# Five gate/up blocks of a hybrid decoder layer: shared products combined with one sum less, on a copied accumulator bank, and four summed pairs in each

## The chip, the cores and the metric

One core of one Trainium2 chip runs the whole layer as one program. The metric is the device time of one execution in microseconds (us); the kernel before took 1085.96 us, the median of three runs (1085.82 to 1085.98).

## What is computed

The reference is one decoder layer for 256 tokens of width 2048 in float32: a normalisation, one combined input projection, a gated linear recurrence beside eight retention heads, an output projection, and a SwiGLU feed-forward part of inner width 5632. The change lies in the feed-forward part:

```python
        h = h + jnp.einsum('bse,ed->bsd', y, w_out[l])
        u = rmsnorm(h, ln2_w[l])
        ff = jax.nn.silu(jnp.einsum('bsd,df->bsf', u, w_ffn_gate[l])) * jnp.einsum('bsd,df->bsf', u, w_ffn_up[l])
        h = h + jnp.einsum('bsf,fd->bsd', ff, w_ffn_down[l])
```

## The kernel before

Every weight is float32 and is split into a high and a low part that TensorE takes at its faster float32 rate (`split`, L110 to L113: ScalarE casts the high part at L112, VectorE subtracts it at L113 for the low part). A product of two split operands is three matmuls (`three`, L667 to L672). So TensorE multiplies three times for each product, and ScalarE and VectorE have to prepare two parts of every weight.

The output projection (blocks 0 and 1), the gate and up projections (blocks 2 to 12) and the down projection are cut into blocks. A gate/up block has two tiles of 128 tokens by two halves of 512 columns (512 gate columns and the matching 512 up columns), so four results, `c11`, `c12`, `c21`, `c22`, each a PSUM bank of 128x512. The depth of 2048 is cut into eight pairs of 128. For one pair the left side is a 2x2 of 128x128 pieces, `a11` to `a22`, and the weights are a 2x2 of 128x512 pieces, `b11` to `b22`.

A plain pair takes eight products (24 matmuls). A summed pair takes seven (21 matmuls), after Strassen and Winograd: VectorE makes four sums of the weight pieces (`Quad.add`, L644 to L648), and four of the seven products are added up over all summed pairs of the block before they are combined. These four are the shared products: `a11 b11`, `s1 t1`, `s3 t3` and `s2 t2`, in the banks `c11`, `c22`, `c21` and `c12` (`Block.share`, L771 to L787). After the last summed pair ScalarE copies the first out (L782), VectorE makes `p` and `q` (L783, L784), ScalarE writes `q` back to `c12` (L785), and VectorE rewrites `c22` and `c21` (L786, L787). Then the three direct products of each summed pair, whose weights are loaded a second time in half (`Direct`, L747), and the plain pairs accumulate onto the four banks.

Each block's work is a word of steps (`STEPS`, L36): `p` is a plain pair of the block itself, `d` the direct products of one of its own summed pairs, and `s` the shared products of one summed pair of the block that follows. So a block's four combined banks are ready before its own first step. `room` (L663) gives even and odd blocks four PSUM banks each in turn. After a block, two banks hold transposes of its result (`turn` in `ffn_post`, L828 to L835), which run during the next block's first step.

`SUMMED` (L32) names the summed pairs: block 3 has three, then 4, 3, 4, 3, 4, 3, 4 from block 4 to block 10, then three in blocks 11 and 12.

Loads go through SyncE's queue, 512 KB each, into six `raw` buffers; the split parts of plain and direct pairs, and of `t1`, `t3`, `b11`, `t2`, go to four pairs of buffers `wh`, `wl`. The program text is written in step order; a scheduler then puts each engine's instructions in an order of its own, and each engine runs its queue in that order. TensorE's rows therefore mix matmuls of two blocks.

Of the kernel before, what the change touches and what calls it, by code (L numbers as in the profile page):

```python
# [14 lines left out]
P = 128  # L15
D = 2048
S = 256
# [14 lines left out]
SUMMED = ((), (4, 5), (2, 3)) + ((1, 2, 3), (0, 1, 2, 3)) * 4 + ((1, 2, 3), (1, 2, 3))  # L32
# [3 lines left out]
STEPS = ("pppspppspp", "ppspdpsdpp", "pdpsdpspspp") + ("pspsdpsdpsdp", "psdpsdpsddp") * 4 + ("psdpsdpsdpp", "psdpsdpsdpp")  # L36


# [6 lines left out]
def tile_hymba_layer(ctx: ExitStack, tc: tile.TileContext, A: dict, out: bass.AP):  # L45
# [491 lines left out]
    class Left:  # L537
# [6 lines left out]
        def __init__(self, f, sums):  # L544
            self.h, self.l = [act_tile("ah", F32R)], [act_tile("al", F32R)]
            split(self.h[0], self.l[0], f)
            if sums:
# [4 lines left out]
                v.tensor_tensor(out=s2, in0=a11, in1=s1, op=ALU.add)  # L552
                v.tensor_tensor(out=s3, in0=a11, in1=a21, op=ALU.subtract)
                v.tensor_tensor(out=s4, in0=a12, in1=s2, op=ALU.subtract)
# [108 lines left out]
    def room(m):  # L663

        return (aux, bank)[m % 2]
# [56 lines left out]

    class Shared(Quad):


        hl = None, None

        def load(self, half):
# [4 lines left out]
            h, l = self.hl  # L733
            if half == 0:
                self.ra = r
                h, l = self.hl = [wpool.tile([P, 1024], F32R, tag=g, name=nm(g)) for g in ("wh", "wl")]
                self.parts["b11"] = h[:, :512], l[:, :512]
                split(*self.parts["b11"], r[:, :512])
                return
            self.add(r)  # L740
            self.parts["t2"] = h[:, 512:], l[:, 512:]
            split(*self.parts["t2"], r[:, :512])
            self.cut(("t1", "t3"), self.ra)
            self.parts["t4"] = act_tile("t4h", F32R), act_tile("t4l", F32R)
            split(*self.parts["t4"], r[:, 512:])
# [16 lines left out]
    class Block:  # L762


        def __init__(self, index, src, lefts, post, steps, summed, before=None):
            self.index, self.src, self.lefts, self.post, self.steps = index, src, lefts, post, steps
            self.summed = summed
            self.shared = [Shared(src(i), True, before and (lambda i=i: before(i))) for i in self.summed]
            self.ps = {}

        def share(self, m):  # L771
            left, right, last = self.lefts[self.summed[m]], self.shared[m].parts, m == len(self.summed) - 1
# [10 lines left out]
            v.tensor_tensor(out=p, in0=ps["c12"], in1=p1, op=ALU.subtract)  # L783
# [91 lines left out]
    def down_block(d, ahead):  # L875
# [15 lines left out]
        def post(c):  # L891
# [4 lines left out]
            elif c == "p7":  # L896
                n = act_tile("n")
                v.tensor_tensor(out=n, in0=ps["p6"], in1=ps["a1"], op=ALU.subtract)
# [303 lines left out]
```

## Time and profile before

| | |
|---|---|
| median of three runs | 1085.96 us |
| span of the profiled execution | 1084.4 us |
| TensorE busy | 1074.2 us (99%) |
| VectorE busy | 953.5 us (88%) |
| ScalarE busy | 660.9 us (61%) |
| first transposes of a block's result, from block 3 on | 437.6, 483.3, 521.7, 567.4, 605.7, 651.5, 689.8, 735.6 us |

The profiled execution's span, from its first to its last instruction, is 1.56 us under the median of the runs. PE is TensorE (PEld its weight loads), ACT ScalarE, DVE VectorE, SP SyncE. In a timeline the first column is the start in us from the span's start, the second the time in us until the end of the group, and the count of merged instructions stands at the end. A matmul's stated duration is from its start to its last result; the next one starts well before that. In the groups of instructions the columns behind the bar are busy time in us and the mean duration of one in ns.

### The profile page before, as it was taken

How to read it: one execution, taken by the hardware profiler on the slowest of the kernel's cores; microseconds unless marked ns; L12 is line 12 of the kernel's file. 1: busy time of each engine (PE TensorE's matmuls, PEld its weight loads, DVE VectorE, ACT ScalarE, POOL GpSimd, SP SyncE). 2: the span in 40 equal slices, each digit the busy share in tenths (PEclk: the TensorE clock that was granted, in tenths of full speed). 3: DMA queues.
4: the chain of work that ended last, by engine and by line, in shares of the span. 5: the costliest groups of instructions: out<-in, count | busy, mean ns of one | idle time of the engine just before them, and what ended most of it. 6: DMA issues, size and time to landing. Idle time of an engine off the chain costs nothing.

```text
span 1084.4 us, 14584 instructions
## 1 busy us (share of the span) xinstructions
PE 1074.2 (99%) x5101; PEld 899.5 (83%) x5101; DVE 953.5 (88%) x1371; ACT 660.9 (61%) x935; POOL 51.0 (5%) x61
## 2 busy tenths in 40 slices
PE   9999999999999999999999999999999999999997
PEld 7888888888888788888888888888888888888885
DVE  7789799988878889888998998999899899898986
ACT  7666644468746676565566566556556666655563
POOL 0612230000000000000000000000000000000001
PEclk9999999999999999999999999999999999999999
DMA  9964474444565567577677677686675756465652
GB/s 330 333 211 168 160 252 173 174 175 171 181 230 205 184 228 275 198 248 266 220 245 261 220 264 235 233 289 214 233 271 194 265 181 213 171 214 199 212 209 85
DMA packets 69274, 238.32 MB, mean 220 GB/s; under 512 B 7888, under 2 KB 8272, under 8 KB 69200
## 3 DMA queue, kind: packets, MB, share of 16 engines
q1 hardware_dynamic: 68400, 235.29, 62.7%
q0 software_dynamic: 512, 1.57, 0.4%
q8 instruction: 40, 0.66, 0.2%
q10 hardware_dynamic: 288, 0.52, 0.1%
q14 instruction: 34, 0.28, 0.1%
HBM read 235.26 MB, written 2.10 MB: 219 GB/s over the span
## 4 chain that ended last, share of the span: by engine, by line
PE 97%; DVE 1%; issue 1%; DMA 0%; ACT 0%; POOL 0%; SPq 0%; POOLq 0%; ACTq 0%
PE c L670 22%; PE c L672 22%; PE c L671 22%; PE fm L184 11%; PE fm L186 5%; PE tm L164 3%; PE tm L165 3%; PE tm L166 3%; PE p L672 1%; PE p L671 1%; PE p L670 1%; PE ft L833 1%; DMA raw<-in_w_v 0%; PE ht L576 0%; PE sc L482 0%
## 5 line engine op out<-in xcount | busy, mean ns | idle before, releaser
L112 ACT CAST wh<-raw 128x1024 fp32r<-128x1024 f32 (+1 forms) x490 | 460.9, 965 | 362.6 <-PE c L672 132.5
L113 DVE TENSOR_TENSOR wl<-raw,wh 128x1024 fp32r<-128x1024 f32 (+1 forms) x490 | 538.2, 1122 | 91.2 <-ACT wh L112 88.4
L671 PE MATMUL c<-wl,ah 128*128 128x512 f32 x850 | 331.0, 390 | 0.0
L672 PE MATMUL c<-wh,al 128*128 128x512 f32 x850 | 330.4, 389 | 0.0
L670 PE MATMUL c<-wh,ah 128*128 128x512 f32 x850 | 275.0, 391 | 0.2 <-ACT wh L112 0.2
L670 PEld LDWEIGHTS c<-wh,ah 128*128 128x128 f32 x850 | 159.4, 188 | 33.4 <-ACT wh L112 1.1
L672 PEld LDWEIGHTS c<-wh,al 128*128 128x128 f32 x850 | 159.6, 188 | 33.0
L671 PEld LDWEIGHTS c<-wl,ah 128*128 128x128 f32 x850 | 159.6, 188 | 32.7
L184 PE MATMUL fm<-u,wh 128*128 128x512 f32 x512 | 161.3, 396 | 0.0
L186 PEld LDWEIGHTS fm<-u,wl 128*128 128x128 f32 x512 | 96.0, 188 | 22.5
L186 PE MATMUL fm<-u,wl 128*128 128x256 f32 x512 | 101.1, 278 | 0.0
L184 PEld LDWEIGHTS fm<-u,wh 128*128 128x128 f32 x512 | 78.4, 189 | 0.3
L648 DVE TENSOR_TENSOR raw<-raw,raw 128x512 f32<-128x512 f32 x106 | 73.1, 690 | 2.8
L648 DVE TENSOR_TENSOR raw<-raw 128x512 f32<-128x512 f32 x106 | 72.7, 689 | 2.4
L671 PE MATMUL c<-wl,sh 128*128 128x512 f32 x176 | 68.5, 389 | 0.0
L672 PE MATMUL c<-wh,sl 128*128 128x512 f32 x176 | 68.0, 389 | 0.0
L670 PE MATMUL c<-wh,sh 128*128 128x512 f32 x176 | 60.4, 394 | 0.3 <-ACT sh L112 0.3
L165 PE MATMUL tm<-wl,u 128*128 128x512 f32 x128 | 48.8, 394 | 0.0
L166 PE MATMUL tm<-wh,u 128*128 128x512 f32 x128 | 48.7, 390 | 0.0
L164 PE MATMUL tm<-wh,u 128*128 128x512 f32 x128 | 47.3, 398 | 0.8 <-ACT u L288 0.8
L954 POOL TENSOR_TENSOR htok<-htok,fw 128x512 f32<-128x512 f32 x2 | 2.5, 1273 | 895.9 <-ACT junk L947 895.9
L670 PEld LDWEIGHTS c<-wh,sh 128*128 128x128 f32 x176 | 33.1, 188 | 7.3 <-ACT sh L112 0.7
(245 smaller groups left out, 1034.9 us busy)
## 6 DMA issues: line engine op xcount, KB each, us to landing
raw<-in_w_gu SPq DMA_DIRECT2D x212, 512.0 KB, 5.5
raw<-in_w_down SPq DMA_DIRECT2D x91, 512.0 KB, 4.3
raw<-in_w_out SPq DMA_DIRECT2D x34, 512.0 KB, 3.7
raw<-in_w_lx SPq DMA_DIRECT2D x16, 512.0 KB, 6.3
raw<-in_w_k SPq DMA_DIRECT2D x16, 512.0 KB, 3.5
raw<-in_w_q SPq DMA_DIRECT2D x16, 512.0 KB, 4.0
raw<-in_w_rg SPq DMA_DIRECT2D x16, 512.0 KB, 3.4
raw<-in_w_lg SPq DMA_DIRECT2D x16, 512.0 KB, 3.4
```

Of the source, the lines that this page charges most:

```text
L112: act.copy(out=dst_h, in_=src)
L113: v.tensor_tensor(out=dst_l, in0=src, in1=dst_h.bitcast(F32), op=ALU.subtract)
L164: pe.matmul(ps, ah, wh, start=first, stop=False)
L165: pe.matmul(ps, ah, wl, start=False, stop=False)
L166: pe.matmul(ps, al, wh, start=False, stop=last)
L184: pe.matmul(ps, wh, hl, start=n + i == 0, stop=False)
L186: pe.matmul(ps[:, :S], wl, hl[:, :S], start=False, stop=n + i == len(order) - 1)
L648: v.tensor_tensor(out=dst, in0=a, in1=b, op=ALU.add)
L670: pe.matmul(p, ah, bh, start=first, stop=False, skip_group_check=onto)
L671: pe.matmul(p, ah, bl, start=False, stop=False, skip_group_check=onto)
L672: pe.matmul(p, al, bh, start=False, stop=last, skip_group_check=onto)
L833: pe.transpose(pt[:, o : o + P], g[:, (2 * b + c) * P : (2 * b + c) * P + P], ident)
```

## The change

It sets four summed pairs in each of blocks 4 to 8 (blocks 5 and 7 had three), and forms the shared products of these five blocks in another way.

In these blocks (`KEEP`) the bank `c22` first takes `a11 b11` of the four summed pairs. After the last of these, ScalarE copies `c22` into a fourth bank, which becomes `c11`; that bank is the one that held the second of the transposes of two blocks earlier (`spare`). Then the four `s2 t2` products are added onto `c22` itself, all at the end, so the split `t2` of each pair is kept in two tiles until then. `s2` has its sign turned, so that `c22` holds the sum that VectorE made before at L783, with the other sign, and ScalarE reads it out as `p` with a scale of -1. The rest, `q` and the three rewrites, is as before. The order of VectorE's sums changes in all shared pairs: `t1`, `t3` are made and split first, then `t2`, then `t4`. In blocks outside `KEEP` the combining is as before, with a sign turned in one instruction (`share_apart`).

```diff
-SUMMED = ((), (4, 5), (2, 3)) + ((1, 2, 3), (0, 1, 2, 3)) * 4 + ((1, 2, 3), (1, 2, 3))
+SUMMED = ((), (4, 5), (2, 3)) + ((1, 2, 3),) + ((0, 1, 2, 3),) * 5 + ((1, 2, 3), (0, 1, 2, 3), (1, 2, 3), (1, 2, 3))
...
+KEEP = tuple(range(4, 9))
...
     class Shared(Quad):
...
+            if self.keep:
+                self.parts["t2"] = act_tile("t2h", F32R), act_tile("t2l", F32R)
             self.parts["t4"] = act_tile("t4h", F32R), act_tile("t4l", F32R)
-            split(*self.parts["t4"], r[:, 512:])
+            b11, b12, b22, b21 = self.ra[:, :512], self.ra[:, 512:], r[:, :512], r[:, 512:]
...
+            def second():
+                add(b12, b12, b22)
+                self.cut(("t1", "t3"), self.ra)
+
+            def third():
+                add(b22, b11, b22)
+                split(*self.parts["t2"], b22)
...
         def share(self, m):
...
+            for c, a, b in (("c22", "a11", "b11"), ("c12", "s1", "t1"), ("c21", "s3", "t3")):
+                if m == 0:
+                    ps[c] = room(self.index)(c)
+                three(ps[c], left[a], right[b], m == 0, last)
+                if last and c == "c22":
+                    ps["c11"], spare[self.index % 2] = seed, None
+                    act.copy(out=seed, in_=ps["c22"])
+            if not last:
+                return
+            for k, i in enumerate(self.summed):
+                three(ps["c22"], self.lefts[i]["s2"], self.shared[k].parts["t2"], False, i == self.summed[-1], True)
+
+            p, q = act_tile("p"), act_tile("q")
+            act.activation(out=p, in_=ps["c22"], func=AF.Copy, scale=-1.0)
+            v.tensor_tensor(out=q, in0=p, in1=ps["c12"], op=ALU.subtract)
+            act.copy(out=ps["c12"], in_=q)
+            v.tensor_tensor(out=ps["c22"], in0=q, in1=ps["c21"], op=ALU.subtract)
+            v.tensor_tensor(out=ps["c21"], in0=ps["c21"], in1=p, op=ALU.subtract)
...
         def turn(b):
             pt = room(j)("ft")
-            for c in range(2):
-                for t, g in enumerate(gated):
-                    o = c * S + t * P
-                    pe.transpose(pt[:, o : o + P], g[:, (2 * b + c) * P : (2 * b + c) * P + P], ident)
+            transposes(pt, [g[:, (2 * b + c) * P : (2 * b + c) * P + P] for c in range(2) for g in gated])
+            if b and j + 4 in KEEP:
+                spare[j % 2] = pt
```

The order of the instructions moves as follows. The places shown belong to block 6, which has four summed pairs before and after; its shared products run during block 5's steps. Numbers in the names are the scheduler's; in the kernel before block 6's banks are `c11_1091`, `c22_1092`, `c21_1093`, `c12_1094`, in the changed one `ft_1105` (the copied bank), `c22_1113`, `c12_1114`, `c21_1115`.

TensorE in the kernel before, around the last of block 6's shared products (the second row is the last `a11 b11`, the fourth the last `s2 t2`, the last but one the first later use of the bank that held `a11 b11`, the last row the first later use of `c22`):

```order
L671 MATMUL c11_1091_5278<-wl_1128_5452,ah_755_3715 128x512 [waits DVE_49]
L672 MATMUL c11_1091_5278<-wh_1127_5451,al_756_3716 128x512
...
L671 MATMUL c12_1094_5290<-wl_1128_5452,sh_758_3724 128x512 [waits DVE_49]
L672 MATMUL c12_1094_5290<-wh_1127_5451,sl_759_3725 128x512
L671 MATMUL c11_1018_4939<-wl_1139_5513,ah_845_4126 128x512 [waits DVE_49]
...
L670 MATMUL c11_1091_5278<-wh_1147_5545,ah_833_4090 128x512 [waits Activation_49]
...
L670 MATMUL c22_1092_5282<-wh_1147_5545,ah_833_4090 128x512 [waits DVE_49]
```

Between the second row and the last but one stand 31 matmuls, and between the fourth and the last row 26.

TensorE in the changed kernel, where block 6's last `a11 b11` (first three rows) meets its first `s2 t2` (fourth row):

```order
L672 MATMUL c22_1113_5326<-b11h_1149_5487,ah_755_3715 128x512 [waits Activation_49]
L673 MATMUL c22_1113_5326<-b11l_1150_5488,ah_755_3715 128x512 [waits DVE_49]
L674 MATMUL c22_1113_5326<-b11h_1149_5487,al_756_3716 128x512
L672 MATMUL c22_1113_5326<-t2h_1094_5254,sh_737_3661 128x512 [waits Activation_49]
L673 MATMUL c22_1113_5326<-t2l_1095_5255,sh_737_3661 128x512
```

No matmul stands between the third row and the fourth, which waits for ScalarE's copy of that bank. Blocks 7 and 8 have the same, with no matmul between; in block 4 it is 19, in block 5 it is 17.

ScalarE in the changed kernel at the same place; the second row is the copy, L825 is `p`:

```order
L114 CAST b11h_1149_5487<-raw_1148_5485 128x512 [waits DMAHW6_49]
L818 COPY ft_1105_5295<-c22_1113_5326 128x512 [waits PE_49]
L114 CAST wh_1156_5499<-raw_1148_5485 128x1024 [waits DVE_49,Activation_49]
L114 CAST wh_1159_5520<-raw_1158_5518 128x1024 [waits DMAHW0_49,Activation_49]
L114 CAST wh_1162_5535<-raw_1161_5533 128x1024 [waits DMAHW1_49,Activation_49]
L114 CAST wh_1165_5541<-raw_1164_5539 128x1024 [waits DMAHW2_49,Activation_49]
```

The casts of the last summed pair's `t1`, `t3` and of the next three loads stand behind the copy.

TensorE in the changed kernel at the end of the shared products (the second row is the last `s2 t2`) up to the first use of the rewritten `c22` (last row):

```order
L673 MATMUL c22_1113_5326<-t2l_1153_5494,sh_758_3724 128x512 [waits DVE_49]
L674 MATMUL c22_1113_5326<-t2h_1152_5493,sl_759_3725 128x512
L673 MATMUL ft_1105_5295<-wl_1171_5577,ah_833_4090 128x512 [waits DVE_49]
L674 MATMUL ft_1105_5295<-wh_1170_5576,al_834_4091 128x512
L672 MATMUL ft_1105_5295<-wh_1173_5591,ah_833_4090 128x512 [waits Activation_49]
L673 MATMUL ft_1105_5295<-wl_1174_5592,ah_833_4090 128x512 [waits DVE_49]
L674 MATMUL ft_1105_5295<-wh_1173_5591,al_834_4091 128x512
L672 MATMUL c22_1113_5326<-wh_1170_5576,ah_833_4090 128x512 [waits DVE_49]
```

Five matmuls stand between, where 26 stood. Block 7 has the same five; block 4 has 30, block 5 has 11, and in block 8 five matmuls are followed by a transpose that waits for VectorE.

VectorE in the kernel before, from the low parts of the last pair's `t1`, `t3` (first row) to the rewrite of `c22` (last row); the third row is the low part of `t2`:

```order
L113 TENSOR_TENSOR wl_1131_5473<-raw_1126_5449,wh_1130_5472 128x1024 [waits Activation_49]
L113 TENSOR_TENSOR wl_1136_5483<-raw_1134_5480,wh_1135_5482 128x1024 [waits DMAHW7_49,Activation_49]
L113 TENSOR_TENSOR wl_1128_5452<-raw_1129_5464,wh_1127_5451 128x512 [waits Activation_49]
L113 TENSOR_TENSOR t4l_1133_5477<-raw_1129_5464,t4h_1132_5476 128x512 [waits Activation_49]
L113 TENSOR_TENSOR wl_1139_5513<-raw_1137_5510,wh_1138_5512 128x1024 [waits DMAHW0_49,Activation_49]
L113 TENSOR_TENSOR wl_1142_5519<-raw_1140_5516,wh_1141_5518 128x1024 [waits DMAHW1_49,Activation_49]
L113 TENSOR_TENSOR wl_1148_5546<-raw_1146_5543,wh_1147_5545 128x1024 [waits DMAHW2_49,Activation_49]
L783 TENSOR_TENSOR p_1144_5535<-c12_1094_5290,p1_1143_5534 128x512 [waits PE_49]
L113 TENSOR_TENSOR wl_1151_5561<-raw_1149_5558,wh_1150_5560 128x1024 [waits DMAHW3_49,Activation_49]
L784 TENSOR_TENSOR q_1145_5536<-p_1144_5535,c22_1092_5282 128x512 [waits DVE_49]
L113 TENSOR_TENSOR wl_1154_5567<-raw_1152_5564,wh_1153_5566 128x512 [waits DMAHW4_49,Activation_49]
L786 TENSOR_TENSOR c22_1092_5282<-q_1145_5536,c21_1093_5286 128x512 [waits DVE_49]
```

VectorE in the changed kernel over the same stretch; the fifth row is the low part of the last `t2`:

```order
L115 TENSOR_TENSOR wl_1157_5500<-raw_1148_5485,wh_1156_5499 128x1024 [waits PE_49,Activation_49]
L115 TENSOR_TENSOR wl_1160_5521<-raw_1158_5518,wh_1159_5520 128x1024 [waits DMAHW0_49,PE_49,Activation_49]
L115 TENSOR_TENSOR wl_1163_5536<-raw_1161_5533,wh_1162_5535 128x1024 [waits DMAHW1_49,PE_49,Activation_49]
L115 TENSOR_TENSOR wl_1166_5542<-raw_1164_5539,wh_1165_5541 128x1024 [waits DMAHW2_49,PE_49,Activation_49]
L115 TENSOR_TENSOR t2l_1153_5494<-raw_1151_5491,t2h_1152_5493 128x512 [waits Activation_49]
L115 TENSOR_TENSOR wl_1171_5577<-raw_1169_5574,wh_1170_5576 128x1024 [waits DMAHW3_49,Activation_49]
L115 TENSOR_TENSOR t4l_1155_5496<-raw_1151_5491,t4h_1154_5495 128x512 [waits Activation_49]
L115 TENSOR_TENSOR wl_1174_5592<-raw_1172_5589,wh_1173_5591 128x1024 [waits DMAHW4_49,Activation_49]
L826 TENSOR_TENSOR q_1168_5568<-p_1167_5567,c12_1114_5330 128x512 [waits Activation_49]
L115 TENSOR_TENSOR b11l_1177_5598<-raw_1175_5595,b11h_1176_5597 128x512 [waits DMAHW5_49,Activation_49]
L828 TENSOR_TENSOR c22_1113_5326<-q_1168_5568,c21_1115_5334 128x512 [waits DVE_49]
```

The last `t2` has moved from behind two low parts of 128x1024 to behind four, and `q` stands at the end with one other instruction between it and the rewrite of `c22`.

In all, TensorE has six matmuls of 128x512 fewer. VectorE has eight sums and six subtractions of 128x512 more and five combining sums fewer. ScalarE has six casts of 128x512 and five copies more, and SyncE two loads more. Over its last 1762 rows TensorE's order is the same as before in everything but the numbers of the names, and over its first 2159 as well.

More of the change, by code (lines that the diff above doesn't have):

```diff
@@ L721, in block, with transposes @@
         program.append((quads[n:], end))
+    spare = [None, None]
+    def transposes(pt, parts):
+        for n, x in enumerate(parts):
+            pe.matmul(
+                pt[:, n * P : n * P + P], x, ident, start=n == 0, stop=True, is_transpose=True, skip_group_check=n > 0
+            )
     class Shared(Quad):
-        hl = None, None
+        keep = False
         def load(self, half):
```

42 lines of the change are left out of this document (30 added, 12 removed).

## Prediction

> **What bounds the kernel now.** I began with the page: its busy times and the chain of work that ended last.
>
> ```profile
> span 1084.4 us, 14584 instructions
> PE 1074.2 (99%) x5101; PEld 899.5 (83%) x5101; DVE 953.5 (88%) x1371; ACT 660.9 (61%) x935; POOL 51.0 (5%) x61
> ...
> PE 97%; DVE 1%; issue 1%; DMA 0%; ACT 0%; POOL 0%; SPq 0%; POOLq 0%; ACTq 0%
> ```
>
> The chain is TensorE's almost alone. A busy TensorE may still be a slow one, so I looked next at its waits and at the pace of its matmuls. First the waits of TensorE in the whole program (us in total, times, longest), then a piece of its timeline in block 4:
>
> ```profile
> PE warm L105 <- DVE eps_t L98: 1.1, 1, 1.1
> PE tm L164 <- ACT u L288: 0.8, 2, 0.5
> PE c L670 <- ACT sh L112: 0.3, 1, 0.3
> PE c L670 <- ACT wh L112: 0.2, 1, 0.2
> ```
> ```profile
> 519.15 0.39 PE L671 MATMUL c<-wl,ah 128*128 128x512 f32 x1
> 519.38 0.39 PE L672 MATMUL c<-wh,al 128*128 128x512 f32 x1
> 519.61 0.39 PE L670 MATMUL c<-wh,ah 128*128 128x512 f32 x1
> 519.83 0.39 PE L671 MATMUL c<-wl,ah 128*128 128x512 f32 x1
> ```
>
> TensorE waits 2.4 us in all, and nowhere in the blocks that change. Its matmuls start (519.83 - 519.15) / 3 = 0.227 us apart and each ends 0.39 us after its start. So a matmul less is worth 0.227 us, and a wait that TensorE does not have today is added to the time in full. Next the four stretches from block to block that hold the steps of blocks 4 to 7 (length, then busy us of PE, PEld, DVE, ACT), and the waits in the part of the program that the change reorders:
>
> ```profile
> 483.30:521.70 38.40, 38.40 (x175) 31.80 (x174) 34.23 (x42) 22.85 (x31) 0.00 (x0) 1.00 0.73 247
> 521.70:567.40 45.70, 45.70 (x207) 37.90 (x206) 41.86 (x52) 27.02 (x36) 0.00 (x0) 1.00 0.71 242
> 567.40:605.70 38.30, 38.30 (x174) 31.75 (x173) 34.14 (x42) 22.77 (x31) 0.00 (x0) 1.00 0.74 247
> 605.70:651.50 45.80, 45.80 (x207) 37.95 (x206) 41.96 (x53) 27.12 (x36) 0.00 (x0) 1.00 0.70 241
> sum 168.20, PE 168.20 PEld 139.41 DVE 152.20 ACT 99.76 POOL 0.00; mean PE 42.05 PEld 34.85 DVE 38.05 ACT 24.94 POOL 0.00
> ```
> ```profile
> ACT wh L112 <- DVE raw L648: 59.4, 22, 3.0
> ACT wh L112 <- PE c L672: 47.8, 42, 2.2
> DVE wl L113 <- ACT wh L112: 21.4, 18, 1.8
> ```
>
> TensorE is busy for the whole 168.20 us; VectorE, at 152.20 us (90%), is the next. ScalarE waits for TensorE 42 times: the two preparing engines run ahead and are held back by full buffers. They bound nothing now, but VectorE has only 16 us to spare here.
>
> **What the change takes away.** Blocks 5 and 7 have one plain pair less and one summed pair more: 24 matmuls become 21, twice. The sum is 6 x 0.227 = 1.4 us less, on the path.
>
> **What it adds beside other work.** The durations:
>
> ```profile
> L113 DVE TENSOR_TENSOR wl<-raw,wh 128x1024 fp32r<-128x1024 f32 x392 | 477.7, 1231 | 78.4 <-ACT wh L112 75.8
> L112 ACT CAST wh<-raw 128x1024 fp32r<-128x1024 f32 x392 | 406.5, 1052 | 324.8 <-DVE raw L648 113.2 <-PE c L672 100.3 <-PE fm L184 47.0
> L648 DVE TENSOR_TENSOR raw<-raw,raw 128x512 f32<-128x512 f32 x106 | 73.1, 690 | 2.8
> L113 DVE TENSOR_TENSOR wl<-raw,wh 128x512 fp32r<-128x512 f32 x98 | 66.9, 683 | 12.7 <-ACT wh L112 12.5
> L112 ACT CAST wh<-raw 128x512 fp32r<-128x512 f32 x98 | 60.4, 617 | 37.7 <-PE c L672 32.2 <-DMA raw<-in_w_v 3.6 <-issue 1.4
> L842 ACT ACTIVATE gated<-c,r_tok 128x512 f32<-128x512 f32 x22 | 13.9, 683 | 1.1 <-PE c L672 1.1
> L844 DVE SCALAR_TENSOR_TENSOR gated<-c,r_tok,gated 128x512 f32<-128x512 f32 x22 | 15.8, 741 | 0.6 <-ACT gated L842 0.6
> L786 DVE TENSOR_TENSOR c<-q,c 128x512 f32<-128x512 f32 x13 | 8.9, 686 | 0.0
> L785 ACT COPY c<-q 128x512 f32<-128x512 f32 x13 | 7.7, 589 | 1.6 <-DVE q L784 1.6
> L782 ACT COPY p<-c 128x512 f32<-128x512 f32 x13 | 7.5, 574 | 0.0
> ```
>
> VectorE gets 8 sums (0.69) and 6 subtractions (0.68) and loses 5 combining sums (0.69): 5.5 + 4.1 - 3.5 = 6.1 us more, against a TensorE that needs 1.4 us less. Put wholly into the four stretches this is 158.3 of 166.8 us, 95%: covered, with half the room left. ScalarE's six casts (0.62) and five copies (0.57 to 0.68) come to some 7 us on 100 of 168: covered. Two more loads of 512 KB ride on DMA engines that are busy 0.70 to 0.74 there: covered. The sign turned at L843 outside the five blocks costs VectorE at most 0.741 - 0.684 us in each of eight places: covered.
>
> **What it adds on the path.** TensorE runs its queue in order, so what counts is how many of its matmuls stand between a result and the first that needs it back through another engine. The steps of such a round trip, from two pieces of timeline (a cast that waited for TensorE and a subtraction that waited for the cast; a matmul that waited for a cast) and VectorE's own pace:
>
> ```profile
> 610.50 0.39 PE L672 MATMUL c<-wh,al 128*128 128x512 f32 x1
> ...
> 610.92 0.62 ACT L112 CAST wh<-raw 128x512 fp32r<-128x512 f32 x1 [2.13 <-PE c L672]
> ...
> 611.58 0.69 DVE L113 TENSOR_TENSOR wl<-raw,wh 128x512 fp32r<-128x512 f32 x1 [1.83 <-ACT wh L112]
> ```
> ```profile
> 370.78 0.61 ACT L112 CAST sh<-s 128x512 fp32r<-128x512 f32 x1
> ...
> 371.44 0.50 PE L670 MATMUL c<-wh,sh 128*128 128x512 f32 x1 [0.30 <-ACT sh L112]
> ...
> 371.78 0.39 PE L671 MATMUL c<-wl,sh 128*128 128x512 f32 x1
> ```
> ```profile
> 515.07 0.69 DVE L786 TENSOR_TENSOR c<-q,c 128x512 f32<-128x512 f32 x1
> 515.67 0.69 DVE L787 TENSOR_TENSOR c<-c,p 128x512 f32<-128x512 f32 x1
> 516.27 0.68 DVE L113 TENSOR_TENSOR wl<-raw,wh 128x512 fp32r<-128x512 f32 x1
> ```
>
> From TensorE's end to ScalarE 0.03, ScalarE to VectorE 0.04, ScalarE to TensorE 0.05; I take 0.05 for VectorE to TensorE too. VectorE starts instructions of this size 0.60 apart. After a wait the next two matmuls start 0.34 apart and not 0.227, so a wait costs 0.11 beside its length.
>
> *The copied bank.* The copy cannot start before the last `a11 b11` has ended, and the first `s2 t2` not before the copy has. From the start of the last matmul: 0.39 + 0.03 + the copy + 0.05. A copy from one PSUM bank to another is not in the trace; the nearest are into PSUM 0.589 and out of it 0.574, and I take 0.58. That makes 1.05, and TensorE would have gone on after 0.227: with the slower start 0.93 us lost. In blocks 4 and 5 the 19 and 17 matmuls between (over 4 us) cover it. In blocks 6, 7 and 8 none stands between: 3 x 0.93 = 2.8 us. What is queued behind the copy on ScalarE are four casts of 128x1024; the first `s2 t2` products are nine matmuls (2.0 us), the first cast is ready 1.05 us after the copy and its low part 1.23 later (2.3), needed at 2.9; the following casts come at 2.1 and 3.2 for needs at 2.5 and 3.9. So I count nothing more there.
>
> *The end of the shared products.* The last `t2`'s low part stands on VectorE behind four low parts of 128x1024, so the last `s2 t2` comes late in TensorE's order, after most other matmuls of that step. Then the chain runs: matmul's end 0.39, 0.03, `p`, 0.04, `q`, the low part of the next `b11`, the rewrite of `c22`, 0.05. `p` is a new form; its bounds are the copy, 0.574, and the ACTIVATE with a vector as scale, 0.683, and I take the copy's, since it has a constant scale. (The Trainium skill, "ScalarE: Activation LUTs", section "What ACT_TABLE_LOAD costs", gives an ACTIVATE with constant scale 186 ns and 0.833 ns an element, and 93 ns more for a vector operand. The rows agree in the difference, 0.683 against 0.589. By the rule `p` is an estimated 0.61, and the four chains that hang on it come to some 0.15 us more in all.) `q` starts at 1.03, the rewrite two starts of 0.60 later, and ends 0.69 after that: 2.92, and TensorE has it at 2.97. With n matmuls between, TensorE gets there at (n + 1) x 0.227. Block 4, n = 30: covered. Block 5, n = 11: 2.72, so 0.25 + 0.11 = 0.36. Blocks 6 and 7, n = 5: 1.36, so 1.61 + 0.11 = 1.72 each. Block 8: after five matmuls a transpose waits for the gating at L844, which is queued behind `q` and one sum: 1.03 + 0.60 + 0.7 + 0.74 + 0.05 = 3.12, so 1.87. Together 0.36 + 3.44 + 1.87 = 5.7 us. In the kernel before, the same chain had 26 matmuls over it.
>
> **The sum.** -1.4 + 2.8 + 5.7 = +7.1 us: the profiled span goes from 1084.4 to 1091.5, and the median, 1.56 above the span, from 1085.96 to 1093.1 us. The bounds: if the slower start after a wait falls away (seven times 0.11) and the VectorE instructions between cost nothing (four times 0.60), 3.2 us less, 1089.9.
>
> **The rivals.** *The waits are over when TensorE gets there* (not slower). The combination occurs 13 times in the kernel before, and TensorE never waited for it; if the engines' lead covered the round trips here as well, only the six matmuls would count: 1085.96 - 1.4 = 1084.6 us. It decides at the point where the rows between take longer than the trip, 1.05 us for the copy and 2.97 for the end. Against it: a lead helps with operands that can be made early, and these come out of TensorE's own last matmul; the rows between are 0 and 5. The Trainium skill, "TensorE: Matmul & The Clock Gate", Part 2, "Step-by-step: what each phase is for", says that TensorE's queue may pull weight loads ahead while the matmuls stay in program order. By that rule no later matmul fills the gap; the matmul that waited at 371.44 above, with nothing run in its place, agrees. Chance 7%.
>
> *VectorE becomes late as well* (slower still). At each copy ScalarE is held until TensorE is done, the lead of both preparing engines is used up, and at 95% VectorE does not win it back, so that TensorE also waits for low parts. If after each of the three uncovered copies one low part of 128x1024 comes a whole subtraction late, that is 3 x 1.23 = 3.7 us more: 1096.8 us. For it: the 16 us to spare halve. Against it: TensorE's own waits give VectorE 7 us back. Chance 15%.
>
> **How the numbers follow.** The forecast, waits of 5 to 9 us against 1.4 us, has 78%; its time is 1093.1. The range reaches from its lower bound, rounded down, to the second rival: 1089.5 to 1097.0. A difference under 0.2%, 2.2 us, cannot be told from none here. The first rival is 0.13% faster and counts mostly as the same: faster 3%, same 6%, slower 91%.
>
> **What would show it.** Right: TensorE's waits in the profile after have new rows, a wait of the first `s2 t2` for ScalarE's copy, three times, some 0.8 us each, and waits for VectorE's rewrite of `c22` in blocks 5, 6 and 7 and its gating in block 8; TensorE has 5095 matmul records or close to it; the stretches of blocks 4 to 8 hold the whole difference and the end of the program is as long as before. Wrong: TensorE without waits there (the first rival), or waits for low parts, `wl` at L115, that exceed those for the copy and the combination (the second).

## The result and the profile after

The changed kernel takes 1093.88 us (median of 4 runs, 1092.71 to 1096.22) beside 1085.97 us before (4 runs, 1085.82 to 1087.17): ratio 1.0075, 95% interval 1.0061 to 1.0089. A second set of five runs, with the experiments below, gave 1093.62 us and 1.0070 (1.0057 to 1.0082). It is slower by 8 us, and the forecast was 1093.1. The profiled run took 1092.71 us.

The page after, with the chain's shares by engine, and then TensorE's waits (us in total, times, longest):

```profile
span 1090.9 us, 14574 instructions
PE 1074.7 (99%) x5095; PEld 897.4 (82%) x5095; DVE 958.5 (88%) x1380; ACT 664.3 (61%) x946; POOL 50.9 (5%) x61
...
PE 96%; issue 1%; DVE 1%; ACT 1%; DMA 0%; POOL 0%; SPq 0%; POOLq 0%; ACTq 0%
```
```profile
PE c L672 <- DVE c L828: 3.0, 2, 1.5
PE c L672 <- ACT ft L818: 2.0, 3, 0.7
PE ft L730 <- DVE gated L903: 1.5, 1, 1.5
```

Six matmuls are gone, and three kinds of wait are new: for the rewrite of `c22` (L828), for the copy into the seed bank (L818), and for block 8's gating (L903). No wait for a low part (L115) has come. The rewrite shows twice here and not three times, since block 5's wait (0.13 us) is too short to be listed. The shares of the page hardly show them: TensorE stands at 99% in both kernels, 1074.7 of 1090.9 us and 1074.2 of 1084.4.

Where the time went is read from the stretches of the blocks that change. The first fence has three of the seven stretches between the first transposes of successive blocks, and the sum, in the changed kernel; the second has the sum of the same seven in the kernel before:

```profile
436.60:481.50 44.90, 44.90 (x204) 37.24 (x203) 40.92 (x51) 27.04 (x37) 0.00 (x0) 1.00 0.72 246
...
524.80:569.30 44.50, 42.36 (x190) 34.40 (x189) 39.59 (x50) 25.62 (x36) 0.00 (x0) 1.00 0.70 237
569.30:613.80 44.50, 42.36 (x189) 34.40 (x188) 39.56 (x50) 25.64 (x36) 0.00 (x0) 1.00 0.71 236
...
sum 305.80, PE 299.19 PEld 245.67 DVE 274.91 ACT 179.24 POOL 0.00; mean PE 42.74 PEld 35.10 DVE 39.27 ACT 25.61 POOL 0.00
```
```profile
sum 298.00, PE 298.00 PEld 247.04 DVE 269.67 ACT 176.21 POOL 0.00; mean PE 42.57 PEld 35.29 DVE 38.52 ACT 25.17 POOL 0.00
```

These stretches are 7.8 us longer: 8.4 us of waits, added up below, less five matmuls (1338 against 1343 records between the first transposes, 1.1 us); the 0.5 us that is left was not placed. What lies ahead of them was 1.0 us shorter (436.6 against 437.6). One matmul of that has moved across the boundary (0.2), and the rest belongs to this run: TensorE did not wait for `u`, as it had for 0.8 us in the trace before. The end is 0.3 us shorter (348.5 against 348.8): 6.5 us of span in all. The two stretches of 44.50 us hold the two full pairs of waits. Here is the copy's wait in block 6 (start, duration, engine, line, operation):

```profile
549.27 0.39 PE L674 MATMUL c<-b11h,al 128*128 128x512 f32 x1
549.70 0.57 ACT L818 COPY ft<-c 128x512 f32<-128x512 f32 x1 [4.61 <-PE c L674]
550.18 2.00 ACT L114 CAST wh<-raw 128x1024 fp32r<-128x1024 f32 x2
550.32 0.50 PE L672 MATMUL c<-t2h,sh 128*128 128x512 f32 x1 [0.66 <-ACT ft L818]
550.65 0.39 PE L673 MATMUL c<-t2l,sh 128*128 128x512 f32 x1
```

The last `a11 b11` starts at 549.27, the first `s2 t2` at 550.32 and not at 549.50: 0.82 late, and the next 0.11 later still. (The 0.66 in brackets counts from the end of the matmul before, 0.39 after its start, where the next would have started 0.227 after it. So a wait costs its bracket, 0.16, and the slower start of 0.11.) And the end of block 6's shared products:

```profile
561.34 0.39 PE L674 MATMUL c<-t2h,sl 128*128 128x512 f32 x1
...
561.76 0.60 ACT L825 ACTIVATE p<-c 128x512 f32<-128x512 f32 x1 [4.72 <-PE c L674]
...
562.39 0.69 DVE L826 TENSOR_TENSOR q<-p,c 128x512 f32<-128x512 f32 x1 [3.03 <-ACT p L825]
...
563.00 0.68 DVE L115 TENSOR_TENSOR b11l<-raw,b11h 128x512 fp32r<-128x512 f32 x1
...
563.60 0.69 DVE L828 TENSOR_TENSOR c<-q,c 128x512 f32<-128x512 f32 x1
...
564.34 0.50 PE L672 MATMUL c<-wh,ah 128*128 128x512 f32 x1 [1.48 <-DVE c L828]
```

From 561.34 to 564.34 are 3.00 us, of which this matmul and the five behind it fill 1.36: the trip that was added up as 2.97.

### The profile page after: what moved, and what is told of

It reads as the page before. It is cut to its first block, busy times and chain, and to the rows that moved or that the text cites. A ratio compares the mean times of both kernels' runs of the same rounds, so it can differ in the third digit from the quotient of the medians.

```text
span 1090.9 us, 14574 instructions
## 1 busy us (share of the span) xinstructions
PE 1074.7 (99%) x5095; PEld 897.4 (82%) x5095; DVE 958.5 (88%) x1380; ACT 664.3 (61%) x946; POOL 50.9 (5%) x61
## 4 chain that ended last, share of the span: by engine, by line
PE 96%; issue 1%; DVE 1%; ACT 1%; DMA 0%; POOL 0%; SPq 0%; POOLq 0%; ACTq 0%
PE c L672 21%; PE c L673 21%; PE c L674 21%; PE fm L186 11%; PE fm L188 5%; PE tm L166 3%; PE tm L167 3%; PE tm L168 3%; PE ft L672 1%; PE ft L673 1%; PE ft L674 1%; PE p L674 1%; PE p L673 1%; PE p L672 1%; PE ft L730 1%
## 5 line engine op out<-in xcount | busy, mean ns | idle before, releaser
L114 ACT CAST wh<-raw 128x1024 fp32r<-128x1024 f32 (+1 forms) x454 | 440.5, 992 | 326.9 <-DVE raw L759 99.3
L115 DVE TENSOR_TENSOR wl<-raw,wh 128x1024 fp32r<-128x1024 f32 (+1 forms) x454 | 514.6, 1156 | 78.4 <-ACT wh L114 71.4
L673 PE MATMUL c<-wl,ah 128*128 128x512 f32 x758 | 295.3, 390 | 0.0
L674 PE MATMUL c<-wh,al 128*128 128x512 f32 x758 | 294.6, 390 | 0.0
L672 PE MATMUL c<-wh,ah 128*128 128x512 f32 x758 | 249.0, 391 | 3.3 <-DVE c L828 3.0
L672 PEld LDWEIGHTS c<-wh,ah 128*128 128x128 f32 x758 | 142.1, 188 | 34.5 <-DVE c L828 4.4
L674 PEld LDWEIGHTS c<-wh,al 128*128 128x128 f32 x758 | 142.3, 188 | 29.5
L673 PEld LDWEIGHTS c<-wl,ah 128*128 128x128 f32 x758 | 142.3, 188 | 29.1
L759 DVE TENSOR_TENSOR raw<-raw,raw 128x512 f32<-128x512 f32 x86 | 59.4, 691 | 2.5
L759 DVE TENSOR_TENSOR raw<-raw 128x512 f32<-128x512 f32 x86 | 59.4, 690 | 2.4
```

Source lines behind the costliest of these rows:

```text
L114: act.copy(out=dst_h, in_=src)
L115: v.tensor_tensor(out=dst_l, in0=src, in1=dst_h.bitcast(F32), op=ALU.subtract)
L672: pe.matmul(p, ah, bh, start=first, stop=False, skip_group_check=onto)
L673: pe.matmul(p, ah, bl, start=False, stop=False, skip_group_check=onto)
L674: pe.matmul(p, al, bh, start=False, stop=last, skip_group_check=onto)
L759: v.tensor_tensor(out=dst, in0=a, in1=b, op=ALU.add)
```

## The experiments

Three theories stood against each other. A: TensorE loses time where too few of its own matmuls stand between a result and its return through another engine. B: VectorE, at 88%, is late. C: the new combination costs by itself. Others came up on the way and are told where they are put to the test. Times are medians; a ratio stands against the kernel before on the same chip.

**The new combining alone.** The pairs and steps of the kernel before:

```diff
-SUMMED = ... ((1, 2, 3),) + ((0, 1, 2, 3),) * 5 + ...
+SUMMED = ... ((1, 2, 3), (0, 1, 2, 3)) * 4 + ((1, 2, 3), (1, 2, 3))
-STEPS = ... ("pspsdpsdpsdp",) + ("psdpsdpsdsdp",) * 4 + ...
+STEPS = ... ("pspsdpsdpsdp", "psdpsdpsddp") * 4 + ...
```

> The new combining (copied bank, accumulation on it, one VectorE sum less) in blocks 4 to 8 with the pairs and the step order of the kernel before. The whole reference is computed. Theory A, the round trips lie uncovered in TensorE's order: in this kernel's order 19 to 27 matmuls stand between the last a11 b11 and the first s2 t2 of every block (5 are needed for 1.05 us), 18 to 30 before the rewritten c22 (13 are needed for 2.97 us) and 35 or more before the transposes, so TensorE has no wait for the copy nor for the combination, and with the 5101 matmuls of the kernel before the time is that of the kernel before, 1086.0 us, +-1. Theory B, VectorE's load: VectorE has less to do than in the kernel before, so 1086.0 us too. Theory C, the new combination costs by itself, whatever stands around it (the changed kernel's 8.4 us over its five blocks): 1094.4 us.

Measured: 1085.91 us, ratio 1.0002 (0.9993 to 1.0011), and no wait of TensorE in the blocks. C falls: the copied bank costs nothing where matmuls stand over it. A and B had forecast the same here.

**The four pairs alone.** The old combining in every block:

```diff
-KEEP = tuple(range(4, 9))
+KEEP = ()
```

> The four summed pairs and the step order of the changed kernel, with the old combining in every block. The whole reference is computed. Theory A: the old combination has 14 matmuls before c12 is needed and 25 before c22 (3.4 and 5.9 us, for chains of about 3.0 and 4.2 us), so no wait is added, and six matmuls are fewer: 1084.6 us. Theory B, VectorE's load: VectorE has five combining sums more than in the changed kernel (3.5 us), so it is later still than there: 1094 us or more, with TensorE waiting for low parts in blocks 4 to 8. Theory C: the new combining is absent, so 1084.6 us.

Measured: 1089.27 us, ratio 1.0031 (1.0019 to 1.0042). A as stated falls here, with C, which had the same figure, and B did not hold either: 4.7 us above the one, 5 under the other. TensorE's waits, and what VectorE did in block 5:

```profile
PE c L672 <- ACT c L845: 1.2, 4, 0.3
...
PE c L672 <- ACT wh L114: 0.7, 4, 0.2
```
```profile
517.58 1.23 DVE L115 TENSOR_TENSOR wl<-raw,wh 128x1024 fp32r<-128x1024 f32 x1 [0.48 <-ACT wh L114]
518.72 0.68 DVE L843 SCALAR_TENSOR_TENSOR p<-c,p 128x512 f32<-128x512 f32 x1
```

`p` could have started at 517.85, when the last `c12` product had ended. It stood behind a low part of 128x1024 until 518.72, and so the copy into `c12` came 0.45 late, with 0.11 for the restart, in each of blocks 5 to 8; a cast came late by 0.44 in each (restart included). That makes 4.0 of the 4.7 us. A trip through VectorE has to include what VectorE is busy with when it begins.

**One exchange of steps.** Both parts of the change, the last shared product a step earlier:

```diff
-STEPS = ... ("psdpsdpsdsdp",) * 4 + ...
+STEPS = ... ("psdpsdpssddp",) * 4 + ...
```

> The changed kernel with one exchange in the order of steps of blocks 4 to 7: the last shared product comes one step earlier, ahead of the direct step that stood before it; both parts of the change are kept, and the whole reference is computed. Theory A: now 16 or 17 matmuls stand over the copy and 19 to 25 over the rewrite of c22 in blocks 5 to 8, 38 or more before the transposes, so all seven waits (8.4 us in the changed kernel's trace) go, and what is left of the change are the six matmuls: 1084.6 us, which is 9.3 us under the changed kernel. Theory B, VectorE's load: its work is the same, and two shared products now follow one another, which asks more of it at once, so 1094 us or more. Theory C: 1094 us.

Measured: 1084.58 us, ratio 0.9988 (0.9979 to 0.9996). Of TensorE's waits only those of the kernel before are left (warm, u, sh, wh). VectorE has as much to do as in the changed kernel:

```profile
PE 1072.7 (99%) x5095; PEld 898.5 (83%) x5095; DVE 959.2 (89%) x1380; ACT 665.3 (61%) x946; POOL 49.9 (5%) x61
```
```profile
545.85 3.90 ACT L114 CAST wh<-raw 128x1024 fp32r<-128x1024 f32 x4 [3.23 <-DVE raw L759]
549.64 0.58 ACT L818 COPY ft<-c 128x512 f32<-128x512 f32 x1
```

So the 8.4 us hang on the order, and neither on VectorE's load nor on the combination. The second fence, block 6's copy on ScalarE, shows a second effect of the exchange: the copy now stands behind the four casts and waits for nothing. In the changed kernel it stood ahead of them.

**The same, with VectorE's work spread.** A plain step between the third and the last shared product:

```diff
-STEPS = ... ("psdpsdpsdsdp",) * 4 + ...
+STEPS = ... ("psdpsdspsddp",) * 4 + ...
```

> As the kernel with the last shared product one step earlier, but with a plain step between the third and the last shared product, so that VectorE's work is spread; the order of the last steps is shared, direct, direct, plain. The whole reference is computed. Theory A: 17 matmuls over the copy, 19 to 25 over the rewrite of c22, 38 or more before the transposes: no waits, 1084.6 us, as there. If VectorE's load counts as a second matter, this one is faster than that with two shared products in a row, by the low parts for which TensorE waits there. Theory B and C: 1094 us.

Measured: 1085.59 us, ratio 0.9996 (0.9987 to 1.0004). A holds to 1 us. The spreading was expected to help if two shared products in a row asked too much of VectorE; it made the time a little worse: in blocks 5, 6 and 7 one cast, held by a sum on VectorE, came 0.17 + 0.11 us late, 0.84 in all.

**The old combining in the good order.** The exchanged steps and

```diff
-KEEP = tuple(range(4, 9))
+KEEP = ()
```

> The four pairs and the step order with the last shared product one step earlier, with the old combining in all blocks. The whole reference is computed. It asks what the new combining is worth once the order covers it. Theory A, only uncovered round trips count: 26 matmuls (6.1 us) stand over the old combination's copy into c12 and 37 (8.6 us) over its rewrite of c22, so no wait, and the time is that of the same order with the new combining, 1084.6 us. Theory B, VectorE is now near its limit, and five combining sums more (3.5 us) show: waits for high and low parts as in the run with the pairs alone, where four of them cost 0.33 + 0.11 us each, so 1.7 us more or above: 1086.3 us or later.

Measured: 1087.64 us, ratio 1.0015 (1.0006 to 1.0023), 3.1 us above the same order with the new combining (2.9 by the ratios, since the chips differ). TensorE waits for casts:

```profile
PE c L672 <- ACT wh L114: 1.1, 5, 0.2
```

Four of them, one in each of blocks 5 to 8, cost 0.38 + 0.11 us, 2.0 us together; the other 1.1 has no row of its own. The casts start 0.11 us after a sum on VectorE has ended, so they were held by it. B holds here: with four pairs the sum saved in the combining is worth its place.

**The copy made twice as long.**

```diff
-                    act.copy(out=seed, in_=ps["c22"])
+                    way = act_tile("way")
+                    act.copy(out=way, in_=ps["c22"])
+                    act.copy(out=seed, in_=way)
```

> The changed kernel with its copy made twice as long: c22 is copied to SBUF and from there into the seed bank, so ScalarE has five copies more and the trip to the first s2 t2 is about 0.6 us longer. The whole reference is computed. The order in which TensorE's matmuls come out is another one: 30 to 36 matmuls stand over the copies in all five blocks (0 in blocks 6, 7 and 8 of the changed kernel), and after the last s2 t2 stand 14, 10, 8 and 6 before the rewritten c22 in blocks 4 to 7, and 6 before c12 in block 8. Theory A, what counts is the order: the three waits for the copy go (2.8 us), and at the ends 2.97 - (n + 1) x 0.227 + 0.11 are lost: nothing in block 4, 0.58, 1.04 and 1.49 in blocks 5 to 7, and in block 8 between 0.9 and 2.6 us, since two gatings and a cast stand on ScalarE ahead of c12's copy. With the six matmuls less: 1088.6 to 1090.3 us, 4 to 5 us faster than the changed kernel although it does more. Theory C, the new combining costs by its own work: the copy doubled costs 3 to 5 x 0.6 us more than the changed kernel: 1095.7 to 1096.9 us.

Measured: 1096.30 us (1093.76 to 1098.84), ratio 1.0090 (1.0074 to 1.0105). The total lies 6 us above A's range. It lies in C's, 1095.7 to 1096.9, but by luck: C has the copy itself cost the time, and no wait for the copy is left. Its terms, from the trace of the run of 1093.76: the waits for the copy went, and the ends in blocks 5, 6 and 7 cost 0.63, 1.08 and 1.53, where 0.58, 1.04 and 1.49 were expected. What had not been counted: block 8's wait for `c12` (3.0 with its restart, 0.9 to 2.6 expected) and, in blocks 5 to 8, waits for casts of 0.49 us and, in three of them, 0.27, 2.8 together.

```profile
PE c L672 <- ACT c L829: 2.7, 1, 2.7
PE c L672 <- DVE c L830: 2.4, 3, 1.3
```

The formula by rows held wherever it was applied to a trip; waits for operands behind it were missing. The runs up to 1098.84 are left for the clock, below.

**Four pairs in blocks 4 to 11.** Made from the exchanged steps:

```diff
-SUMMED = ... ((0, 1, 2, 3),) * 5 + ((1, 2, 3), (0, 1, 2, 3), (1, 2, 3), (1, 2, 3))
+SUMMED = ... ((0, 1, 2, 3),) * 8 + ((1, 2, 3),)
-STEPS = ... ("psdpsdpssddp",) * 4 + ...
+STEPS = ... ("psdpsdpssddp",) * 7 + ("psdpsdpsddp", "psdpsdpsdpp")
-KEEP = tuple(range(4, 9))
+KEEP = tuple(range(4, 12))
```

> The kernel with the last shared product one step earlier, carried on: four summed pairs, the new combining and that step order in blocks 4 to 11, so blocks 9 and 11 lose one plain pair each too. The whole reference is computed. TensorE has 5089 matmuls, and 16 or more stand over every copy and 19 or more over every c22. Theory A: six matmuls less again, 1.4 us: 1083.2 us. Theory B: VectorE's further 6 us of sums and subtractions show as waits of TensorE for high and low parts in blocks 8 to 11, as 0.28 us a block did in the run with the spread steps: 1084.3 us or later, and no gain over the kernel that it is made from.

Measured: 1085.17 us, ratio 0.9991 (0.9982 to 1.0000): no gain over its parent. Most of what the six matmuls save, 1.4 us, was given back by one wait for a cast in block 12's time, 0.92 us in brackets and 1.2 with its two additions. So B's figure was met, but not where B had it: there is no wait in blocks 8 to 11.

```profile
PE c L672 <- ACT wh L114: 1.1, 2, 0.9
```

**The changed kernel again.**

> The changed kernel as it is, once more, for its time beside the experiments: its profiled run was at 1092.7 us, its other three between 1093.8 and 1096.2. Six matmuls less and the 8.4 us of waits in its trace make 1086.0 - 1.4 + 8.4 = 1093.0 us; if its median is again 1093.9, about 0.9 us come from something that the one trace does not hold.

Measured: 1093.62 us (1092.90 to 1095.22). The profiled run is the one of 1095.22, and it holds what the first trace did not. TensorE after block 8's wait, and the window behind it (the eighth column is the granted clock):

```profile
654.31 0.44 PE L730 MATMUL ft<-ident,gated 128*128 128x128 f32 x2 [2.07 <-DVE gated L903]
...
655.06 0.63 PE L674 MATMUL c<-wh,al 128*128 128x512 f32 x1
655.48 0.63 PE L672 MATMUL c<-wh,ah 128*128 128x512 f32 x1
...
658.04 0.58 PE L672 MATMUL c<-wh,ah 128*128 128x512 f32 x1
658.46 0.39 PE L673 MATMUL c<-wl,ah 128*128 128x512 f32 x1
658.69 0.39 PE L674 MATMUL c<-wh,al 128*128 128x512 f32 x1
```
```profile
655.00:658.40 3.40, 3.40 (x9) 2.68 (x9) 3.40 (x6) 0.62 (x1) 0.00 (x0) 0.50 0.01 2
```

From 655.06 to 658.46 eight matmuls start 0.425 us apart, at half the clock: 3.40 us for 1.82 us of work, 1.6 lost. The wait itself was 0.5 longer than in the first trace (2.07 against 1.54), since a load came later and held a cast for 3.17 us (2.25 there), and VectorE's sums ahead of `q` moved with it:

```profile
649.59 0.62 ACT L114 CAST wh<-raw 128x512 fp32r<-128x512 f32 x1 [3.17 <-DMA raw<-in_w_gu]
```

With 8.4 us as in the first trace, 1086.0 - 1.4 + 8.4 + 0.5 + 1.6 = 1095.1 us; measured 1095.22.

**TensorE in the written order.** In the changed kernel's steps, TensorE's matmuls of the last shared product keep the order of the code:

```diff
-                    run = lambda m=m: after.share(m)
+                    def run(m=m):
+                        hold = m == len(after.summed) - 1 and after.index in KEEP
+                        with tc.manual_schedule(engines={nc.tensor.engine}) if hold else ExitStack():
+                            after.share(m)
```

> The changed kernel with the same steps, pairs and instructions, but with TensorE's matmuls of the last shared product of each of the blocks 4 to 8 kept in the order in which the code writes them. The whole reference is computed. Then 8 to 19 matmuls stand over the copy in every block, 12 before the rewritten c22 in blocks 5 and 7, 20 and 19 in blocks 6 and 8, and 35 before block 8's transposes. In the changed kernel's trace the last t2's low part was ready at 556.50 us in block 6, and TensorE took it up at 561.11, so most of its place in the order was not asked for by the data. Theory A, the order alone: the waits go but for some 0.1 us in blocks 5 and 7, and the time is 1084.6 to 1084.9 us. Theory D, the late place was needed: in the written order the last s2 t2 stands 15 matmuls (3.4 us) earlier in blocks 6 and 8, TensorE reaches t2's low part before VectorE has it, and waits for that in place of c22, up to 1 us a block: 1086 to 1089 us.

Measured: 1092.90 us, ratio 1.0062 (1.0050 to 1.0075). A, taken as rows alone, failed by 8 us, and D was right that operands come late, but not on which: not `t2`'s low part, but `t1`'s and `t3`'s high parts, and the time lies 4 us above its range. Block 6, a sum on VectorE (two instructions; the first writes `t1`, `t3`'s source), then ScalarE, then TensorE:

```profile
548.66 1.42 DVE L759 TENSOR_TENSOR raw<-raw,raw 128x512 f32<-128x512 f32 x2
```
```profile
550.69 0.57 ACT L818 COPY ft<-c 128x512 f32<-128x512 f32 x1 [4.64 <-PE c L674]
551.17 2.95 ACT L114 CAST wh<-raw 128x1024 fp32r<-128x1024 f32 x3
```
```profile
550.26 0.39 PE L674 MATMUL c<-b11h,al 128*128 128x512 f32 x1
552.27 0.49 PE L672 MATMUL c<-wh,sh 128*128 128x512 f32 x1 [1.62 <-ACT wh L114]
553.22 0.50 PE L672 MATMUL ft<-wh,ah 128*128 128x512 f32 x1 [0.45 <-ACT wh L114]
```

The source was there at 549.35, but the casts stood on ScalarE behind the copy, which waited 4.64 us for TensorE's last `a11 b11`. TensorE, held to the written order, needed the cast right after that product, and lost 1.78 and 0.72 us, and 0.11. The same happened in block 8, with a stretch of half clock behind it (1.6 us). In block 7 of the same run, and in block 5, ScalarE has the copy behind the four casts, and no cast came late:

```profile
592.27 3.91 ACT L114 CAST wh<-raw 128x1024 fp32r<-128x1024 f32 x4 [3.42 <-DVE raw L759]
596.08 0.57 ACT L818 COPY ft<-c 128x512 f32<-128x512 f32 x1
```

Those blocks lost 0.17 us each, at the rewrite of `c22`, near the 0.1 that A had forecast. The late casts and the clock make 2 x 2.6 + 1.6 = 6.8 of the 8.3 us by which this kernel is slower than the one with the exchanged steps.

**The copy on VectorE.** Made from the kernel in the written order. This tests theory Q, that the queue behind the copy is the cause:

```diff
-                    act.copy(out=seed, in_=ps["c22"])
+                    v.tensor_copy(out=seed, in_=ps["c22"])
```

> The kernel with TensorE's written order in the last shared products, with the copy of c22 into the seed bank on VectorE instead of ScalarE. The whole reference is computed. It asks whether the two waits of 1.8 and 0.7 us for high parts there, in blocks 6 and 8, come from what stood behind the waiting copy on ScalarE's queue. Theory Q, the queue: ScalarE is no longer held, so the casts of t1 and t3 are done in time and no wait for high parts is left in blocks 5 to 8; in its place the low parts stand behind the copy on VectorE's queue in all four blocks: from the start of the last a11 b11 0.44 to the copy, 0.6 for it, 0.6 for a sum, 1.23 for the low part and 0.05, 2.9 us, and TensorE gets there after 6 x 0.227 in blocks 6 and 7 and 4 x 0.227 in blocks 5 and 8: waits for low parts of about 1.6 and 2.0 us, twice each, 7 to 8 us in all: 1092 us and, if the clock drops, 1.7 us more each time. Theory S, the sums come late by themselves: the waits for high parts in blocks 6 and 8 stay as long as they were, whatever engine copies.

Measured: 1092.89 us, ratio 1.0061 (1.0047 to 1.0075). The waits for casts went in block 6 (0.2 left of 2.5), and the low part behind the copy on VectorE came late instead:

```profile
PE c L673 <- DVE wl L115: 3.6, 3, 1.4
...
PE c L672 <- ACT wh L114: 0.9, 2, 0.7
PE ft L672 <- ACT wh L114: 0.9, 2, 0.5
```

With restarts it cost 1.34 and 1.66 us in blocks 6 and 7, 1.39 in block 5; 1.6 and 2.0 had been expected. Q does not hold for all blocks: block 5 waited 0.62 us for a cast as well, and in block 8 waits for casts of 0.87 and 0.72 stayed (1.78 and 0.72 with the copy on ScalarE). What holds the cast there is VectorE's sum, as theory S has it:

```profile
638.76 0.69 DVE L759 TENSOR_TENSOR raw<-raw,raw 128x512 f32<-128x512 f32 x1
639.56 3.90 ACT L114 CAST wh<-raw 128x1024 fp32r<-128x1024 f32 x4 [3.42 <-DVE raw L759]
```

The sum now starts 0.81 us ahead of the last `a11 b11`, where it started 1.56 ahead with the copy on ScalarE, and the cast starts 0.11 after the sum has ended. In block 6 the sum moved the other way, from 1.60 ahead to 2.69, so part of the gain there may be the sum's. By the rows of the written order, without the copy the cast of block 6 could have started at 549.46 and not at 551.17, so an estimated 1.7 of the 1.78 us was the queue's. The median agrees with Q's 1092 us in part by luck, since its trace has a stretch of half clock in block 5 (1.6 us) and low parts that came less late than expected.

**Block 12 as well.** The kernel with four pairs in blocks 4 to 11, and

```diff
-KEEP = tuple(range(4, 12))
+KEEP = tuple(range(4, 13))
```

> The kernel with four pairs in blocks 4 to 11, with the new combining in block 12 (three pairs) as well. The whole reference is computed. There TensorE had one wait left, 0.92 us for a cast in block 12's time, at 815.2 us of its trace, where VectorE prepares the left sides of the last products and the old combination side by side. Theory A: the new combining takes one VectorE sum out of that place and lets the wait shrink to 0.3 us: 1083.5 to 1084.5 us. Theory B: the wait has another cause (a buffer, a load) and stays: 1085.0 us as there, +-0.3.

Measured: 1084.01 us (1083.07 to 1085.06), ratio 0.9980 (0.9971 to 0.9989), the fastest of all, and faster than both kernels. Theory A's 1083.5 to 1084.5 us was met: the wait of 0.92 is gone, with VectorE at 89%. The order of ScalarE's and VectorE's rows changed there too, so that it was the one sum is likely, not shown:

```profile
PE 1071.5 (99%) x5089; PEld 897.4 (83%) x5089; DVE 965.0 (89%) x1390; ACT 669.2 (62%) x956; POOL 50.0 (5%) x61
```

**The copy twice, a second trace.**

> The kernel with the copy made twice as long, once more, for a second trace: its five runs were between 1093.8 and 1098.8 us, and the mean granted clock was 0.998 in the two shortest and 0.995 or 0.996 in the three longest. Theory E, a wait of over about 2 us can drop TensorE's clock to half for 3.4 us, as after the wait of 2.07 us in the second trace of the changed kernel, and costs 1.7 us each time that it happens: a run of 1095 us or more shows such stretches in its trace, 1.7 us each above 1093.8, and a run near 1094 shows none. Otherwise the longer runs have longer waits at an unchanged clock.

Measured: 1093.99 and 1094.65 us, and the trace of the run of 1093.99 shows no stretch of half clock. That agrees with E, but no run over 1095 us of this kernel was caught in a trace, so that its longest runs are due to the clock is likely (their mean clock was 0.995 and 0.996, against 0.998 in the two shortest), not shown.

## Why the prediction was right, and where not

*The sum.* Its terms against the first trace: the copy 2.8 forecast, 2.79 measured (0.93 in each of blocks 6, 7 and 8, nothing in 4 and 5); the end in block 5 0.36 against 0.40, in blocks 6 and 7 1.72 against 1.76 each, in block 8 1.87 against 1.70; together 8.5 against 8.4. Six matmuls less: 5095 records. The time was right because each term was, but for block 8, 0.17 too long.

*The form of `p`.* Taken as a copy's 0.574 us; it took 0.598:

```profile
L825 ACT ACTIVATE p<-c 128x512 f32<-128x512 f32 x5 | 3.0, 598 | 19.3 <-PE c L674 19.3
L818 ACT COPY ft<-c 128x512 f32<-128x512 f32 x5 | 2.9, 573 | 13.6 <-PE c L674 13.6
```

So the estimate by the Trainium skill ("ScalarE: Activation LUTs", section "What ACT_TABLE_LOAD costs"), 0.61, was the nearer one; it is 0.02 us a chain. The copy from bank to bank took 0.573 (0.58 forecast).

*What was covered.* VectorE's and ScalarE's additional work was, as the waits after and the exchanged steps show; by the page it is 5.0 and 3.4 us of busy time, where 6.1 and some 7 had been added up from durations. But "half the room left" was too easy a reading: with 3.5 us more (the old combining) in the exchanged order TensorE did wait, 0.49 us in each of four blocks. VectorE's mean load had room; the stretch around the last shared product had little.

*The cause of the late `s2 t2`.* The prediction put it down to the low part behind four others on VectorE. That was wrong as an account of the chip: in block 6 that low part was ready at 556.50, and its matmul ran at 561.11. Why the scheduler put it so late stays open. What an earlier end lacks, in the written order, are the casts behind the copy on ScalarE (blocks 6 and 8). "I count nothing more there" held for the time, because the order that the change brings has other matmuls in that place; where TensorE is held to the early order, the late casts cost 2.6 us a block, of which an estimated 1.7 is the queue's.

*The clock.* This term was missing. It is in one of the two traces of the changed kernel. Whether it also accounts for the 0.9 us by which the first median lay above 1093.0 is not shown. Another candidate is the wait for `u` ahead of the blocks, which changes from trace to trace: none and 0.4 us in the changed kernel's two.

*The rivals.* The waits were not over when TensorE arrived. VectorE, the second rival, did not become late in the changed kernel.

## What to carry to other kernels

Where one engine is the bound and runs in order, a new trip through another engine is priced by the rows between result and return, and a different order of steps, with the same work, can be worth more than the work saved: here +8 us became -1.4. Count as well what stands behind the waiting instruction on the other engine, and what that engine is in the middle of when the trip begins. A wait of the bound engine can be followed by a stretch at a lower clock, so a kernel with waits of 2 us can take longer in one run than in another: here 1.6 of the 2.5 us between the two traced runs.

## What the runs showed of the hardware

TensorE's clock halved after waits of 2.07 us (changed kernel, second trace), of 1.62 + 0.45 us (written order, block 8) and of 0.44 + 1.10 us (copy on VectorE, block 5), each time for some 1.6 us of loss. The stretches of the second and the third (clock in the eighth column):

```profile
640.50:643.90 3.40, 3.40 (x9) 2.61 (x9) 3.40 (x5) 2.87 (x4) 0.00 (x0) 0.51 0.74 220
510.60:514.00 3.40, 3.40 (x10) 2.64 (x8) 3.40 (x4) 1.66 (x2) 0.00 (x0) 0.51 0.73 247
```

It did not halve after a wait of 1.54 us (first trace), nor of 2.7 and 2.3 us (the copy twice, both traces), nor after the same 1.62 + 0.45 us in block 6 of the written order. So the length of the waits alone doesn't decide it. The Trainium skill, "TensorE: Matmul & The Clock Gate", Part 1, "What's actually happening", gives an activity window of 3.4 us that runs freely, and half the clock after an idle one. The half-clock stretch of 3.40 us agrees with the window's length, and that the same wait halves the clock in one run and not in another agrees with its running freely. The waits here are shorter than the window, so a whole idle window isn't needed. Here the measurement differs from the page's rule, and it decides.
